# Turned blocks through GpSimd's DMA queue, convolution taps spread over chunks, block-product loads in place: a decoder trunk on one core

## The chip, the cores and the metric

The kernel runs on one core of one Trainium2 chip. The metric is the device time of a whole execution in microseconds. Three executions of the kernel before took 2344.26, 2345.53 and 2347.45 us; their median, 2345.53 us, is the time before. The profile is of one more execution, with its own time, given below.

## The reference, cut to what matters

A decoder trunk of two layers on 256 tokens (BATCH = 1, SEQ = 256, D_MODEL = 2048). Layer 0 mixes tokens by gated linear attention, layer 1 by forgetting attention; both attend to 256 memory tokens besides. After each comes the channel mixer, the part that the change is about: a gated MLP with a hidden width of 5632 and a causal convolution of width 3 over the tokens ahead of the gate.

```python
def causal_dwconv(u, w, b):
    s_ = u.shape[1]
    up = jnp.pad(u, ((0, 0), (CONV_WIDTH - 1, 0), (0, 0)))
    return w[0] * up[:, 0:s_] + w[1] * up[:, 1:s_ + 1] + w[2] * up[:, 2:s_ + 2] + b

def conv_ffn(h, w_up, conv_w, conv_b, w_down):
    u = causal_dwconv(h @ w_up, conv_w, conv_b)
    a, val = split_cols(u, [FFN_HIDDEN, FFN_HIDDEN])
    return (jax.nn.silu(a) * val) @ w_down

def reference(x, mem, norm_mix, norm_ffn, ...):
    mem_n = rmsnorm(mem, norm_mem)
    for i in range(DEPTH):
        ...
        h = rmsnorm(x, norm_ffn[i])
        x = x + conv_ffn(h, ffn_w_up[i], ffn_conv_w[i], ffn_conv_b[i], ffn_w_down[i])
    return rmsnorm(x, norm_final)
```

All inputs are float32.

## The kernel before, in words

**Products.** Every float32 factor is split in two halves, hi (rounded) and lo (the rest), and a product is made of three matmuls: hi by hi, lo by hi, hi by lo. Weights come from memory in units of 128 x 1024 (512 KB): SyncE (SP) issues the load into `raw` (L225), ScalarE (ACT) casts it to `whi` (L230), VectorE (DVE) subtracts to get `wlo` (L231). There are four buffers of each. These steps are issued with high priority, so they run ahead of the rest by as much as the buffers allow.

**The channel mixer.** `ffn` works through the hidden width in three parts (`PARTS`) of 16, 16 and 12 chunks of 128. In each part up panels come first, then down panels over the part's chunks. A panel made by `pair_tm` (L373) has 16 units k = 0 to 15 of weights (12 in the last part's down panel). An up panel (`up_pair`) makes four hidden chunks, as two "turned blocks" of two chunks each; the last four chunks of the third part are made by two single panels (`up`, by way of `panel_tm`, 8 units), one turned block each. A down panel (`down_pair`) takes the part's chunks as input and makes two of the four column blocks of the output, f = 0 or 2; so each of the first two parts ends with panels f=0 and f=2, the last with f=0 and the products of `add_out`.

**Block products.** Two units k and k+1 for which `sums` has an entry are multiplied as a 2 x 2 product of blocks with seven products in place of eight. In up panels this is k = 4 (`SEVEN_UP`), in the down panels of the first two parts it is given by `SEVEN_DOWN`. It needs both units at once in `raw2` (two buffers, loads at L391), differences of the weight blocks on DVE (L397 to L400), and its own casts and low halves (L349, L350), and sums of the input blocks (`token_sums`, tiles `usum` and `dsum`). The loads at L391 are issued with high priority and no other tie.

**A turned block.** Up products leave tokens on the partitions; the convolution wants channels there. DVE scales and adds (L1407) and transposes 32 x 32 blocks (L1382). Then `far_away` (L601) writes the tile of 512 KB to DRAM (L603, the profile's `far<-yu` or `far<-yzu`), and `back` reads it in four DMAs of 128 KB (L608, `fvt<-far` or `yzu<-far`), which put the 32 x 32 blocks in place. All are issued by SP. Two buffers are there for each side (`ys`, `zs`).

**The convolution.** `convolve` reads a turned block z: twelve ACT instructions of 128 x 256 (L1347, L1348, L1349, one of each for each of four quarters), two adds on DVE (L1352), SiLU on ACT (L1353), the product with the gate's other half on DVE (L1355, tile `cv`), and the split of the result into the hi and lo halves of `m` (ACT L484, DVE L485), from which the down panels multiply (tiles `mix`, `A`, `B` in the profile). For a chunk in `SEVEN_DOWN`, `token_sums` follows.

**What sets the order.** Each engine runs its instructions in one fixed order, which a scheduler makes from priorities: work written later comes later, unless it stands under `high_priority`; `issue_after(x)` keeps an instruction behind x. Up panels write their turned blocks to DRAM when they end. `close(left)` does the rest, and is called from hooks at given units: it issues the four reads behind the last load so far, then the whole `convolve`, with DVE's part behind the last `wlo` so far. An up panel closes the two blocks of the panel before it after units 7 and 11; a down panel f=0 those of the last up panel after units 7 and 9; the last part's down panel closes what is open after unit 4; the single panels close one at a time.

## Time and profile before

| | |
|---|---|
| median of three executions | 2345.53 us |
| profiled execution, its own time | 2346.2 us |
| its span | 2344.3 us |
| mean granted clock of TensorE | 0.981 |
| TensorE busy | 2247.9 us (96%) |
| VectorE busy | 1790.5 us (76%) |
| ScalarE busy | 1425.3 us (61%) |
| GpSimd busy | 3.3 us, 15 instructions |

A line of the profile names an engine, the line of the kernel, and what it writes and reads (out<-in). Engines are PE (TensorE, matmuls), PEld (its loads of weights, which overlap), DVE (VectorE), ACT (ScalarE), POOL (GpSimd) and SP (SyncE, whose DMA queue is written SPq). Buffer names are shared by several uses: a turned block that has come back is `fvt` in layer 0 and `yzu` in layer 1. TensorE is busy nearly all the time, so a stretch is judged by how far it is longer than its matmuls need, and by the clock that the throttle granted there (1.00 is full speed). A panel of 16 units can be cut out of the span by the start of its first matmul and that of the next panel's first.

### The profile page before, as it was taken

The page shows a single profiled execution, that of the slowest core. Times are in us where ns is not written, and L with a number is a line of the kernel's source. Part 1 is how long each engine was busy: PE and PEld are TensorE (multiplying, and loading weights), DVE is VectorE, ACT ScalarE, POOL GpSimd, SP SyncE. Part 2 cuts the span into 40 slices and gives each one's busy share as a digit, 9 for nine tenths or more (in the row PEclk, how much of TensorE's full clock was granted, in tenths as well). Part 3 has the DMA queues.
Part 4 walks back from the last instruction along what each step waited for, and adds up shares of the span by engine and source line. Part 5 has one row for each costly group of instructions (what it writes and reads, how often), then busy time and mean ns, then how long its engine had stood idle before and what let it go on. Part 6 is the DMA issues. An engine that isn't in the chain of part 4 may idle for free. (4 is left out here: it accounts for less than half of the span.)

```text
span 2344.3 us, 29896 instructions
## 1 busy us (share of the span) xinstructions
PE 2247.9 (96%) x10317; PEld 1869.6 (80%) x10317; DVE 1790.5 (76%) x2639; ACT 1425.3 (61%) x2258; POOL 3.3 (0%) x15
## 2 busy tenths in 40 slices
PE   9999999999979999799999999999997999899997
PEld 7889888878768777687788998877786878778776
DVE  7668887678878689777687579677897868887856
ACT  6655665557755576656674555556765566754674
POOL 0000000000000000000000000000000000000000
PEclk9999999999989999899999999999998999999998
DMA  9777657867755667566788667677675666756683
GB/s 343 230 219 219 197 190 253 255 203 242 226 183 189 219 216 242 162 216 196 242 255 241 207 208 249 199 242 236 208 247 157 219 203 228 225 179 219 203 256 135
DMA packets 183488, 513.37 MB, mean 219 GB/s; under 512 B 20636, under 2 KB 66344, under 8 KB 183336
## 3 DMA queue, kind: packets, MB, share of 16 engines
q1 hardware_dynamic: 182760, 510.66, 68.8%
q8 instruction: 81, 1.33, 0.2%
q10 hardware_dynamic: 576, 0.79, 0.1%
q14 instruction: 71, 0.58, 0.1%
HBM read 468.63 MB, written 42.74 MB: 218 GB/s over the span
## 5 line engine op out<-in xcount | busy, mean ns | idle before, releaser
L231 DVE TENSOR_TENSOR wlo<-raw,whi 128x1024 fp32r<-128x1024 f32 (+4 forms) x734 | 868.5, 1197 | 343.6 <-ACT whi L230 326.2
L230 ACT ACTIVATE whi<-raw 128x1024 fp32r<-128x1024 f32 (+4 forms) x734 | 751.5, 1039 | 491.2 <-PE acc L334 184.8
L334 PE MATMUL acc<-whi,B 128*128 128x512 f32 (+3 forms) x1376 | 323.9, 371 | 0.0
L334 PEld LDWEIGHTS acc<-whi,B 128*128 128x128 f32 x1376 | 251.1, 188 | 33.1
L349 ACT ACTIVATE whi<-raw 128x1024 fp32r<-128x1024 f32 (+1 forms) x144 | 137.2, 953 | 198.4 <-DVE raw L398 62.4
L373 PE MATMUL acc<-whi,mix 128*128 128x512 f32 x850 | 232.0, 409 | 9.6 <-ACT whi L230 8.3
L350 DVE TENSOR_TENSOR wlo<-raw,whi 128x1024 fp32r<-128x1024 f32 (+1 forms) x144 | 155.7, 1082 | 77.1 <-ACT whi L349 73.7
L373 PEld LDWEIGHTS acc<-whi,mix 128*128 128x128 f32 x850 | 168.9, 200 | 49.3 <-ACT whi L230 10.2
L373 PE MATMUL acc<-whi,B 128*128 128x512 f32 x730 | 191.1, 394 | 8.6 <-ACT whi L230 3.7
L334 PE MATMUL acc<-wlo,B 128*128 128x512 f32 (+3 forms) x688 | 176.0, 371 | 0.0
L373 PEld LDWEIGHTS acc<-whi,B 128*128 128x128 f32 x730 | 138.5, 190 | 39.7 <-ACT whi L230 4.8
L334 PEld LDWEIGHTS acc<-wlo,B 128*128 128x128 f32 x688 | 126.6, 188 | 16.9
L1352 DVE TENSOR_TENSOR tap<-tap,tap 128x1024 f32<-128x1024 f32 x88 | 107.4, 1221 | 18.7 <-ACT tap L1348 12.8
L373 PE MATMUL acc<-wlo,mix 128*128 128x512 f32 x425 | 121.4, 391 | 0.0
L373 PE MATMUL acc<-wlo,B 128*128 128x512 f32 x365 | 105.1, 393 | 0.1
L373 PEld LDWEIGHTS acc<-wlo,mix 128*128 128x128 f32 x425 | 80.7, 190 | 17.3
L373 PE MATMUL ps_s<-whi,mix 128*128 128x512 f32 x334 | 94.2, 394 | 0.0
L373 PE MATMUL ps_s<-whi,B 128*128 128x512 f32 x342 | 94.0, 390 | 0.0
L334 PE MATMUL acc<-whi,mix 128*128 128x512 f32 x336 | 84.2, 390 | 0.0
L373 PEld LDWEIGHTS acc<-wlo,B 128*128 128x128 f32 x365 | 69.0, 189 | 15.4 <-DVE wlo L350 0.5
L373 PEld LDWEIGHTS ps_s<-whi,B 128*128 128x128 f32 x342 | 64.2, 188 | 13.7
L373 PEld LDWEIGHTS ps_s<-whi,mix 128*128 128x128 f32 x334 | 63.3, 190 | 13.7
(417 smaller groups left out, 3670.7 us busy)
## 6 DMA issues: line engine op xcount, KB each, us to landing
raw<-wp SPq DMA_DIRECT2D x743, 512.0 KB, 4.4
fvt<-far SPq DMA_DIRECT2D x100, 128.0 KB, 4.6
raw<-wp SPq DMA_DIRECT2D x32, 384.0 KB, 3.5
yzu<-far SPq DMA_DIRECT2D x96, 128.0 KB, 4.4
far<-yu SPq DMA_DIRECT2D x22, 512.0 KB, 3.4
far<-yzu SPq DMA_DIRECT2D x22, 512.0 KB, 3.4
raw<-wp SPq DMA_DIRECT2D x24, 388.0 KB, 3.7
far<-blk SPq DMA_DIRECT2D x12, 512.0 KB, 4.7
```

Source lines behind the costliest of these rows:

```text
L230: casts.append(S.activation(hi[:, s], raw[:, s], AF.Copy))
L231: lows.append(V.tensor_tensor(lo[:, s], raw[:, s], hi[:, s].bitcast(F32), ALU.subtract))
L334: mm = TE.matmul(acc[b][:, :n], src[kc - base][:, part, b * P : (b + 1) * P], ready[low][:, j * n : (j + 1) * n], start=i == low == part = ...
L349: casts.append(S.activation(hi[:, :n], src, AF.Copy))
L350: lows.append(V.tensor_tensor(lo[:, :n], src, hi[:, :n].bitcast(F32), ALU.subtract))
L373: r = TE.matmul(bank[name], x, w, start=name not in begun, stop=last)
L1352: V.tensor_tensor(t, t, taps[i_][:, :, :, :T], ALU.add)
```

## The change

- `far_away` takes a queue. In the channel mixers the write and the four reads of a turned block are issued on GpSimd's queue, all at once when the block is turned; elsewhere they stay on SP. In all 44 writes and 176 reads move. Blocks of the single panels land in a tile of their own, with the buffers of `raw2`.
- `convolve` is cut into six steps: `taps_of` for each quarter (three ACT instructions, kept behind the last cast so far), `add_taps`, `gated` (their DVE instructions kept behind the last `wlo` so far). A turned block puts its steps in a list `waiting` with the unit from which each may run, 8 units after the block was turned (7 for single panels). `tick(most)` counts units and runs up to `most` steps that are due; up panels run one and two in turn, the others two a unit. A down panel runs down what is left: at most six steps are open after unit 11 of 16, none after unit 13 (7 and 9 of 12 in the last part).
- The loads of a block product stay behind the last load so far.
- The down panels' second block product is that of units 10 and 11, where it was 8 and 9.
- Hooks become one function that is called at every unit; after a block product it is called for both of its units. A closure that nothing called goes away.

The matmuls and the arithmetic of every engine are the same, but for which pair of units is the second block product.

```diff
--- before.py
+++ after.py
@@ -33,7 +33,7 @@
 PARTS = ((0, 16), (16, 32), (32, 44))
 WIDE = ((0, 4, 8, 12), (16, 20, 24, 28), (32, 36))
 SEVEN_UP = (4,)
-SEVEN_DOWN = (4, 8)
+SEVEN_DOWN = (4, 10)
 
 
 LEVELS = (64, 16, 4)
@@ -350,7 +350,7 @@
             lows.append(V.tensor_tensor(lo[:, :n], src, hi[:, :n].bitcast(F32), ALU.subtract))
         return hi, lo
 
-    def pair_tm(units, src, sums, flip, pool, early, late, hooks={}):
+    def pair_tm(units, src, sums, flip, pool, early, late, hook):
 
         bank = {}
         fast, slow = ("p1", "p5", "p7", "p6"), ("p2", "p3", "p4", "x")
@@ -358,6 +358,7 @@
         tags = {n: ("acc", 4) for n in accs}
         tags.update(zip(works, (("o", 1), ("s", 2), ("s", 2), ("t", 1))))
         begun = set()
+        sums = dict(sums)
         n = len(units)
         plan = []
         k = 0
@@ -387,8 +388,9 @@
             if k in sums:
                 with tc.high_priority(offset=AHEAD):
                     ra, rb = [pool.tile([P, NUNIT], F32, name="raw2", tag="raw2", bufs=2) for _ in range(2)]
-                    for t, (off, _, w) in ((ra, units[k]), (rb, units[k + 1])):
-                        loads.append(nc.sync.dma_start(t, wp[off : off + P * w].rearrange("(p n) -> p n", p=P)))
+                    with tc.issue_after(loads[-1].ins):
+                        for t, (off, _, w) in ((ra, units[k]), (rb, units[k + 1])):
+                            loads.append(nc.sync.dma_start(t, wp[off : off + P * w].rearrange("(p n) -> p n", p=P)))
                 st = [[sums[k][:, part, j, :] for part in range(2)] for j in (3, 0, 1, 2)]
                 done = k == end[-1]
                 w1 = split_more(ra[:, :512], 512)
@@ -409,7 +411,8 @@
                 last_mm.append(three("p4", tok(k + 1, 1), [t[:, :512] for t in w4]))
                 if done:
                     early(bank)
-                hooks.get(k + 1, int)()
+                hook(k)
+                k += 1
             else:
                 w = split_unit(units[k])
                 last = k == n - 1
@@ -423,7 +426,7 @@
                         ends.append(r)
                         late(b, h, bank[name])
                 last_mm.append(r)
-            hooks.get(k, int)()
+            hook(k)
 
     def token_sums(r, dst):
 
@@ -597,15 +600,15 @@
                 (nc.scalar if on_act(q, c) else nc.sync).dma_start(
                     dst[32 * c : 32 * (c + 1), q], src[32 * q : 32 * (q + 1), c])
 
-    def far_away(pool, src, n):
+    def far_away(pool, src, n, queue=nc.sync):
 
         far = pool.tile([P, 4 * T], F32, name="far", tag="far", bufs=3)
-        nc.sync.dma_start(far[:, : 4 * n], src[:, : 4 * n])
+        queue.dma_start(far[:, : 4 * n], src[:, : 4 * n])
         blocks = far[:, : 4 * n].rearrange("(q i) (c n) -> c i q n", q=4, c=4)
 
         def back(dst):
             for c in range(4):
-                nc.sync.dma_start(dst[32 * c : 32 * (c + 1), : 4 * n].rearrange("i (q n) -> i q n", q=4), blocks[c])
+                queue.dma_start(dst[32 * c : 32 * (c + 1), : 4 * n].rearrange("i (q n) -> i q n", q=4), blocks[c])
 
         return back
 
@@ -1277,7 +1280,7 @@
                     steps[f](u)
 
 
-    def down_pair(l, p, f, src, sums, flip, pool, temps, then=None, hooks={}):
+    def down_pair(l, p, f, src, sums, flip, pool, temps, hook, then=None):
 
         def early(bank):
             t0, t1 = temps()
@@ -1296,7 +1299,7 @@
             if then is not None:
                 then(f + h, b)
 
-        pair_tm(where["down", l, p, f], src, sums, flip, pool, early, late, hooks)
+        pair_tm(where["down", l, p, f], src, sums, flip, pool, early, late, hook)
 
     def add_out(key, src, then=None, spare=None, last=None, first=0, hooks=None, late=1):
 
@@ -1331,33 +1334,40 @@
             for i in (1, 2):
                 nc.gpsimd.memset(taps[i][:, :, :, :i], 0.0)
             count = [0, 0, 0]
-            open_ = []
             sums = {}
 
             def held(name, i):
                 return fp.tile([P, 2, 4, P], F32R, name=name, tag=f"{name}{i}")
 
-            def convolve(j, i, z, seven):
-
-                for s in range(2):
-                    for c in range(2):
-                        col = (c * 44 + j + s) * 4
-                        w = [cw[:, col + n : col + n + 1] for n in range(4)]
-                        src = z[:, :, 2 * c + s]
-                        S.activation(by_run(taps[0][:, s, c, :]), src, AF.Identity, bias=w[3], scale=w[2])
-                        S.activation(by_run(taps[1][:, s, c, 1:]), src, AF.Copy, scale=w[1])
-                        S.activation(by_run(taps[2][:, s, c, 2:]), src, AF.Copy, scale=w[0])
+            def taps_of(j, s, c, z):
+
+                col = (c * 44 + j + s) * 4
+                w = [cw[:, col + n : col + n + 1] for n in range(4)]
+                src = z[:, :, 2 * c + s]
+                with tc.issue_after(casts[-1].ins):
+                    S.activation(by_run(taps[0][:, s, c, :]), src, AF.Identity, bias=w[3], scale=w[2])
+                    S.activation(by_run(taps[1][:, s, c, 1:]), src, AF.Copy, scale=w[1])
+                    S.activation(by_run(taps[2][:, s, c, 2:]), src, AF.Copy, scale=w[0])
+
+            def add_taps():
+
                 t = taps[0]
-                for i_ in (1, 2):
-                    V.tensor_tensor(t, t, taps[i_][:, :, :, :T], ALU.add)
+                with tc.issue_after(lows[-1].ins):
+                    for n in (1, 2):
+                        V.tensor_tensor(t, t, taps[n][:, :, :, :T], ALU.add)
                 S.activation(t[:, :, 0, :], t[:, :, 0, :], AF.Silu)
+
+            def gated(i, seven):
+
+                t = taps[0]
                 r = fp.tile([P, 2, T], F32, name="cv", tag="cv")
-                V.tensor_tensor(r, t[:, :, 0, :], t[:, :, 1, :], ALU.mult)
-                for s in range(2):
-                    split(m, i + s, r[:, s, :])
-                if seven:
-                    sums[i] = held("dsum", i)
-                    token_sums(r, sums[i])
+                with tc.issue_after(lows[-1].ins):
+                    V.tensor_tensor(r, t[:, :, 0, :], t[:, :, 1, :], ALU.mult)
+                    for s in range(2):
+                        split(m, i + s, r[:, s, :])
+                    if seven:
+                        sums[i] = held("dsum", i)
+                        token_sums(r, sums[i])
 
             def input_sums(k):
 
@@ -1372,24 +1382,36 @@
             def scale(b):
                 return nx.col()[:, b : b + 1]
 
-            def turn(j, i):
+            def turn(j, i, wait, z=None):
 
                 count[0] += 1
                 y = ys[count[0] % 2]
+                z = zs[count[0] % 2] if z is None else z
 
                 def evac(b, a):
                     with tc.high_priority(offset=AHEAD):
                         V.transpose(y[:, :, :, b, :], a.rearrange("p (k c i) -> p c k i", c=4, i=32))
                     if b:
-                        back = far_away(dram, flat(y), T)
-                        open_.append((j, i, back))
+                        far_away(dram, flat(y), T, nc.gpsimd)(flat(z))
+                        steps = [lambda s=s, c=c: taps_of(j, s, c, z) for s in range(2) for c in range(2)]
+                        steps += [add_taps, lambda: gated(i, j < PARTS[-1][0] and i in SEVEN_DOWN)]
+                        waiting.extend((clock[0] + wait, step) for step in steps)
 
                 return evac
 
-            def up_pair(j, i, hooks):
+            waiting, clock = [], [0]
+
+            def tick(most):
+
+                clock[0] += 1
+                for _ in range(most):
+                    if waiting and waiting[0][0] <= clock[0]:
+                        waiting.pop(0)[1]()
+
+            def up_pair(j, i, hook):
 
                 count[2] += 1
-                turns = [turn(j + 2 * h_, i + 2 * h_) for h_ in range(2)]
+                turns = [turn(j + 2 * h_, i + 2 * h_, 8) for h_ in range(2)]
                 u = {}
 
                 def early(bank):
@@ -1407,11 +1429,11 @@
                     V.scalar_tensor_tensor(u[b, h_], a, scale(b), u[b, h_], ALU.mult, ALU.add)
                     turns[h_](b, u[b, h_])
 
-                pair_tm(where["up", l, j], h, up_sums, count[2] % 2, pool, early, late, hooks)
+                pair_tm(where["up", l, j], h, up_sums, count[2] % 2, pool, early, late, hook)
 
             def up(j, i):
 
-                done = turn(j, i)
+                done = turn(j, i, 7, pool.tile([P, 4, 4, 2, 32], F32, name="turn2", tag="raw2", bufs=2))
 
                 def evac(b, a):
                     t = temps(b)
@@ -1420,50 +1442,39 @@
 
                 return panel_tm(("up", l, j), h, evac)
 
-            def close(left):
-
-                while len(open_) > left:
-                    j, i, back = open_.pop(0)
-                    z = zs[count[1] % 2]
-                    count[1] += 1
-                    with tc.issue_after(loads[-1].ins):
-                        back(flat(z))
-                    with tc.issue_after(lows[-1].ins):
-                        convolve(j, i, z, j < PARTS[-1][0] and i in SEVEN_DOWN)
-
-            def closing(*at):
-                return {k: lambda left=len(at) - 1 - i: close(left) for i, k in enumerate(at)}
-
-            def take_first():
-                nx.take()
-                for k in SEVEN_UP:
-                    input_sums(k)
+            def first(k):
+                {2: lambda: nx.land(landing[0]), 3: nx.take, 8: nx.col,
+                 9: lambda: nx.land(landing[1]), 11: nx.take}.get(k, int)()
+                tick(0)
 
             for p, (lo, hi) in enumerate(PARTS):
+                end = p == len(PARTS) - 1
                 for j in WIDE[p]:
-                    hooks = closing(7, 11)
                     if p == 0 and j == lo:
                         for k in SEVEN_UP:
                             input_sums(k)
-                        hooks = {2: lambda: nx.land(landing[0]), 3: nx.take, 8: nx.col,
-                                 9: lambda: nx.land(landing[1]), 11: nx.take}
-                    up_pair(j, j - lo, hooks)
+                    up_pair(j, j - lo, first if p == 0 and j == lo else lambda k: tick(1 + clock[0] % 2))
                 for j in range(lo, hi, 2):
                     if j in WIDE[p] or j - 2 in WIDE[p]:
                         continue
                     step = up(j, j - lo)
                     for u in range(8):
                         step(u)
-                        if u in (2, 5):
-                            close(max(1, len(open_) - 1))
-                end = p == len(PARTS) - 1
+                        tick(2)
                 for f in (0,) if end else (0, 2):
-                    hooks = {4: lambda: close(0)} if end else closing(7, 9) if f == 0 else {}
-                    if end:
-                        hooks[6] = getattr(then, "begin", int)
                     count[2] += 1
+
+                    def hook(k):
+                        tick(2)
+                        if k in (hi - lo - 5, hi - lo - 3):
+                            left = 6 if k == hi - lo - 5 else 0
+                            while len(waiting) > left:
+                                waiting.pop(0)[1]()
+                        if end and k == 6:
+                            getattr(then, "begin", int)()
+
                     down_pair(l, p, f, m, {} if end else sums, count[2] % 2, pool, lambda: (temps(0), temps(1)),
-                              then if end else None, hooks)
+                              hook, then if end else None)
                 sums.clear()
             add_out(("down", l, len(PARTS) - 1), m, then=then, first=2, spare=spare, last=last)
 
```

## The prediction

> **What bounds the kernel now.** First the page's head and first part, then the windows cut at the panel borders, then the waits of TensorE (columns of the waits: total us, times, longest us).
>
> ```profile
> span 2344.3 us, 29896 instructions
> PE 2247.9 (96%) x10317; PEld 1869.6 (80%) x10317; DVE 1790.5 (76%) x2639; ACT 1425.3 (61%) x2258; POOL 3.3 (0%) x15
> ```
>
> TensorE is the bound, so only its idle time and its slow clock can be won: the change removes no matmul. Two panels without a convolution run free of stalls and give the floor of a panel.
>
> ```profile
> 701.10:743.70 42.60, 42.60 (x188) 35.09 (x187) 37.06 (x45) 20.55 (x22) 0.00 (x0) 1.00 0.62 200
> 743.50:786.60 43.10, 43.10 (x191) 35.60 (x190) 28.80 (x31) 21.29 (x24) 0.00 (x0) 1.00 0.62 197
> ```
>
> The first is a down panel (f=2), the second an up panel: length, busy time of PE, PEld, DVE, ACT, POOL, then granted clock, 1.00 in both. Against them stand the panels in which a convolution runs: the four down panels f=0 of the first two parts (first row below, sum of the four), the fourteen up panels after the first of each part's start (first, last, sum), and the two down panels of the last parts.
>
> ```profile
> 640.00:701.20 61.20, 49.05 (x188) 38.38 (x187) 47.77 (x60) 34.39 (x55) 0.00 (x0) 0.86 0.60 187
> ...
> sum 239.40, PE 192.37 PEld 151.90 DVE 186.49 ACT 136.32 POOL 0.00; mean PE 48.09 PEld 37.98 DVE 46.62 ACT 34.08 POOL 0.00
> ```
>
> ```profile
> 505.80:551.20 45.40, 43.52 (x191) 35.58 (x190) 36.27 (x42) 33.89 (x54) 0.00 (x0) 1.00 0.67 213
> ...
> 2169.20:2216.90 47.70, 45.58 (x193) 37.10 (x192) 37.66 (x45) 34.62 (x54) 0.00 (x0) 0.96 0.62 199
> sum 638.80, PE 615.30 PEld 500.23 DVE 525.75 ACT 469.69 POOL 0.00; mean PE 43.95 PEld 35.73 DVE 37.55 ACT 33.55 POOL 0.00
> ```
>
> ```profile
> 1156.80:1195.70 38.90, 35.11 (x146) 27.99 (x145) 25.84 (x31) 27.24 (x49) 0.00 (x0) 0.96 0.74 230
> 2259.80:2302.80 43.00, 37.83 (x146) 30.17 (x145) 24.08 (x29) 25.79 (x46) 0.00 (x0) 0.88 0.68 221
> ```
>
> Excess over the floor: f=0, 239.4 − 4×42.6 = 69.0; up, 638.8 − 14×43.1 = 35.4; last parts, 81.9 − 2×42.6×146/188 = 15.7 (scaled by the matmul records). Together 120 us, the most that this change can touch. The waits name what ends the stalls: casts of the weights on ACT, above all those of the block products (L349).
>
> ```profile
> PE ps_t L373 <- ACT whi L349: 23.8, 8, 5.8
> PE ps_s L373 <- ACT whi L349: 23.6, 6, 6.4
> PE ps_o L373 <- ACT whi L230: 14.5, 8, 2.5
> PE acc L373 <- ACT whi L230: 12.0, 6, 3.1
> ```
>
> Why the casts are late shows in the timeline of the panel at 640.0, ACT first (start, length, idle before and its releaser), then SP.
>
> ```profile
> 655.93 0.60 ACT L1347 ACTIVATE tap<-fvt,cw 128x256 f32<-128x256 f32 x1 [2.00 <-DMA fvt<-far]
> ...
> 659.81 0.59 ACT L1347 ACTIVATE tap<-fvt,cw 128x256 f32<-128x256 f32 x1
> 660.30 1.04 ACT L349 ACTIVATE whi<-raw 128x1024 fp32r<-128x1024 f32 x1
> ...
> 672.77 0.52 ACT L1348 ACTIVATE tap<-fvt,cw 128x256 f32<-128x256 f32 x1 [3.80 <-DMA fvt<-far]
> ...
> 675.98 1.04 ACT L349 ACTIVATE whi<-raw 128x1024 fp32r<-128x1024 f32 x1
> ```
>
> ```profile
> 648.68 1.52 SPq L603 DMA_DIRECT2D far<-yu  x2
> 651.31 1.77 SPq L608 DMA_DIRECT2D fvt<-far  x4
> 655.79 7.19 SPq L391 DMA_DIRECT2D raw<-wp  x2
> 663.03 1.55 SPq L608 DMA_DIRECT2D fvt<-far  x2
> ```
>
> Ten taps stand before the cast at 660.30, eight before that at 675.98; ACT itself first waited 2.00 and 3.80 us for the turned block, and the second block's reads waited on SP behind two loads for a block product that held the queue 7.19 us. What TensorE lost by it, and what the clock then added:
>
> ```profile
> 661.40 1.22 PE L373 MATMUL ps_t<-whi,dsum 128*128 128x512 f32 x2 [4.85 <-ACT whi L349]
> 677.08 2.08 PE L373 MATMUL ps_s<-whi,dsum 128*128 128x512 f32 x4 [4.66 <-ACT whi L349]
> ```
>
> ```profile
> 675.60:685.80 10.20, 7.64 (x17) 5.57 (x18) 7.32 (x9) 9.22 (x15) 0.00 (x0) 0.50 0.37 108
> ```
>
> After such a stall the granted clock is 0.50 for some us. In the last part's panel the taps themselves come late and TensorE waits behind them:
>
> ```profile
> 1164.72 0.60 ACT L1347 ACTIVATE tap<-fvt,cw 128x256 f32<-128x256 f32 x1 [4.70 <-DMA fvt<-far]
> ...
> 1171.00 3.43 PE L373 MATMUL acc<-whi,mix 128*128 128x512 f32 x8 [3.15 <-ACT whi L230]
> ```
>
> **The change, part by part.** The order of the changed program has the same matmuls, casts, taps and DVE instructions, in the same forms; only order and queues differ. The sum is made against the profiled run's own time, 2346.2 us (span 2344.3, so 1.9 around it); the median of the runs shown is 2345.53.
>
> *Turned blocks on POOL's queue.* The 44 far writes and 176 reads leave SP and are issued by POOL as soon as a block is turned. On SP that frees 220 issues; SP is no bound, and gains only in that weight loads never stand behind a waiting read. What an issue on POOL takes, no row shows: POOL has 15 instructions and no DMA. The nearest rows are SP's own issues and the DVE instruction for which POOL might have to wait:
>
> ```profile
> L608 SPq DMA_DIRECT2D fvt<-far x100: 302/430/1367, 514.9 to 1222.0; - x100
> L231 DVE TENSOR_TENSOR wlo<-raw,whi 128x1024 fp32r<-128x1024 f32 (+4 forms) x734 | 868.5, 1197 | 343.6 <-ACT whi L230 326.2 <-PE acc L334 5.6 <-PE acc L259 2.7
> ```
>
> Lower bound 0.43 us (the median), then 0.43 + 1.2 = 1.6, and 0.43 + 2×1.2 = 2.8 if two DVE instructions hold each issue. I take about 1 us, between the first two, with no row nearer. What it may cost: from the first write's issue (648.68, panel start + 8.7) to the first tap (655.93) a block took 7.25 us on SP, so it is in place at + 16. Six more issues are in its way now (two writes, four reads of the block before), each g − 0.43 longer. In the new order ACT casts units 6 to 9 first and comes to the taps near + 19 (seven units of 43.1/16 = 2.7 each). Twelve taps take 5.2 us: from 655.93 to 659.81 nine of them start, one every 0.43. The cast behind them is that of unit 10, which TensorE reaches at 10×2.7 = 27, near + 28 with the stall of unit 4 before it. So a landing up to 28 − 5.2 = + 22.8 costs nothing: (22.8 − 16)/6 + 0.43 = 1.56 us an issue. Above that each microsecond more costs six per panel.
>
> The wait for the write now stands on POOL, behind which only other blocks queue. On the Trainium skill's page "SBUF — State Buffer", section "Who interferes with whom", DVE in a two-port mode locks GpSimd out of SBUF, and its note on the "DVE blocks DMA" trap says that descriptors for a GpSimd DMA then can't be written; tensor_tensor is said to have no such mode. No run here shows POOL's DMA beside DVE yet. By that page these panels, whose DVE rows are tensor_tensor, scalar_tensor_tensor and transposes, would be free of the lock, and the sum stays as it is.
>
> *Convolution spread, block product (4,8) to (4,10), in the f=0 panels.* The first two long stalls (4.85, 4.66) go: taps stand behind casts of coming units. What is late next is DVE and the splits of the last chunks: chunks 12 to 15 of this panel are still made in it, and their splits stand later than before, since their convolution starts 8 ticks after the turn. DVE's work bounds the panel from below: 46.62 us mean, 4 over the floor; from above the old 59.85 (239.4/4). Following the new order with these durations I find about 1 us at unit 4, 1 at unit 10, 4 at unit 12 and 2 to 4 at unit 14, and one slow-clock stretch of 1.5 (3.4 us at half): 53 us, midway between the bounds. Gain 4 × (59.85 − 53) = 27.4; bounds 0 and 53.
>
> *The same in up panels.* The mean excess is 35.4/14 = 2.5 us. The burst of taps no longer precedes a due cast, but DVE's subtractions for the block product at unit 4 follow older convolution work on DVE (37.55 of 45.6 us busy): 1.5 us stays. Gain 14 × 1.0 = 14; bounds 0 and 35.4.
>
> *Last parts.* The reads no longer wait for the hook after unit 4, so the taps come before the cast that waited 3.15 us; a stall of 1.8 stays where chunk 10's split stands behind the next cast, and part of the slow clock. Gain 15.7 − 2×3 = 9.7; bounds 0 and 15.7.
>
> *The single panels' block tile.* It takes a buffer of the block products' loads; after the last pair panel of a layer no block product follows in that mixer, so nobody waits for it: 0.
>
> *Loads for block products in order.* They are issued later than now, but still about four units (11 us) before their use, and a load lands 4.4 us after issue: no cost while those 6 us cover it.
>
> ```profile
> raw<-wp SPq DMA_DIRECT2D x743, 512.0 KB, 4.4
> ```
>
> Sum: 2346.2 − 27.4 − 14 − 9.7 = 2295.1 us.
>
> **The rivals.**
> 1. *POOL's issues are slow* (the other side). At 2.4 us an issue a block lands at 16 + 6×1.97 = + 27.8, 5.0 late: 2.5 over the old 2.5 in fourteen up panels is 35, a half-clock stretch of 1.5 in each is 21, the other gains are lost: 2346 + 56 = 2402. It decides from about 2.2 us, where 14 × 6 × (g − 1.56) eats the 51 gained. For it: no POOL DMA in the trace, and DVE is busy 78% of the f=0 panels (46.62 of 59.85), so an issue that needs DVE to pause waits often. Against it: 10 issues in 43 us leave 4 us for each.
> 2. *The stall only moves to DVE.* Casts of a block product follow DVE's subtractions already; if DVE's order sets the f=0 panels, only 2 us each go there and little elsewhere: 2346 − 10 = 2336. For it: 46.62 us of DVE in 42.6 of matmuls. Against it: DVE idles 13 us in these panels today.
> 3. *All the stalls go.* With DVE's 46.62 left in f=0 and the last parts as forecast: 2346 − 53 − 35 − 10 = 2248. For it: every long wait named ends in an ACT cast. Against it: the late splits above.
> 4. *The change doesn't do what it says*: POOL's reads land no earlier than SP's did, since the write's landing is waited for either way. Then only the 7.19 us hold on SP goes, near 2330; it is in rival 2's chance.
>
> **How the numbers follow.** Forecast 2295 (2278 to 2315): 0.42. Rival 3: 0.11. Rivals 2 and 4: 0.22, of which 0.12 is faster, 0.05 within 0.2% (about what a measurement of this kernel can tell from no change), 0.05 slower. Rival 1: 0.25, all slower. So faster 0.65, same 0.05, slower 0.30. The range goes from rival 3 to between no change and rival 1's time, 2248 to 2385; above it lie POOL issues near 2.4 us and more.
>
> **What would show it.** Right: the f=0 panels near 53 us with no wait over 4.9 on L349; up panels near 44.6; the last parts' near 36; issues on POOL of about 1 us; first taps without idle for a block; half-clock stretches fewer. Wrong: taps that idle for their block in up panels (rival 1); f=0 panels of 57 us or more with DVE busy nearly throughout (rival 2); waits on loads for block products.

## The result and the profile after

Four executions of the changed kernel took 2288.9 to 2291.38 us, median 2289.98; the kernel before, beside it, 2345.8. The ratio is 0.976 with a 95% interval of [0.9745, 0.9779]: faster by 56 us, where 2295.1 was forecast. The profiled execution took 2289.51 us. Its head and first part, from the page:

```profile
span 2287.7 us, 30031 instructions
PE 2230.5 (97%) x10317; PEld 1861.7 (81%) x10317; DVE 1790.0 (78%) x2639; ACT 1416.9 (62%) x2258; POOL 124.3 (5%) x235
```

TensorE has the same 10317 matmuls and is busy 17 us less; since the matmuls are the same, that is taken here as less of the half clock (the mean granted clock rose from 0.981 to 0.990). The other 39 us of the 56.6 by which the span is shorter were its idle time. The windows at the panel borders, cut as in the prediction (length, busy time of PE, PEld, DVE, ACT, POOL, granted clock), first for the four f=0 panels:

```profile
636.10:684.70 48.60, 45.33 (x188) 35.71 (x187) 45.77 (x61) 34.37 (x55) 5.50 (x10) 0.96 0.66 225
...
sum 200.80, PE 183.55 PEld 145.42 DVE 182.12 ACT 135.27 POOL 21.99; mean PE 45.89 PEld 36.35 DVE 45.53 ACT 33.82 POOL 5.50
```

for the fourteen up panels (two of them and the sum):

```profile
505.00:548.10 43.10, 43.10 (x191) 35.62 (x190) 37.02 (x43) 32.67 (x52) 5.63 (x10) 1.00 0.72 236
...
591.30:636.30 45.00, 43.48 (x191) 35.53 (x191) 39.49 (x48) 33.05 (x54) 5.49 (x10) 1.00 0.70 237
...
sum 614.40, PE 607.30 PEld 497.93 DVE 530.07 ACT 464.63 POOL 77.06; mean PE 43.38 PEld 35.57 DVE 37.86 ACT 33.19 POOL 5.50
```

and for the down panels of the two last parts:

```profile
1124.80:1169.90 45.10, 37.29 (x146) 29.93 (x146) 26.01 (x31) 27.54 (x50) 2.74 (x5) 0.89 0.59 189
2203.60:2246.10 42.50, 34.99 (x146) 28.21 (x145) 25.41 (x30) 27.68 (x50) 2.74 (x5) 0.92 0.62 211
```

Against the panels of before: f=0 239.4 to 200.8 (-38.6), up 638.8 to 614.4 (-24.4), last parts 81.9 to 87.6 (+5.7). The waits of TensorE (total us, times, longest) say what is left:

```profile
PE acc L374 <- ACT B L487: 9.3, 2, 6.5
PE acc L374 <- ACT whi L349: 8.2, 6, 1.6
PE acc L374 <- ACT A L487: 4.6, 2, 2.8
PE ps_s L374 <- ACT whi L349: 4.2, 3, 2.8
PE acc L374 <- ACT fvt L1440: 3.9, 1, 3.9
PE acc L374 <- ACT mix L487: 3.9, 1, 3.9
PE ps_t L374 <- ACT whi L349: 3.0, 5, 1.6
...
PE ps_o L374 <- ACT whi L349: 2.2, 1, 2.2
```

Two rows of before, beside those that the prediction shows:

```profile
PE acc L373 <- ACT whi L349: 3.9, 4, 1.8
...
PE ps_o L373 <- ACT whi L349: 2.0, 2, 1.5
```

The 47.4 us that ps_t and ps_s waited for casts of block products (L349) have shrunk to 7.2; on acc and ps_o these waits grew from 5.9 to 10.4. Together 53.3 became 17.6. As much again, 17.8 in these rows, are now waits for splits of the convolution's result (L487), and these are the longest that are left (6.5); 3.9 is for an evacuation (L1440). ACT's timeline shows how an f=0 panel runs now (start, length, idle before):

```profile
649.19 3.89 ACT L230 ACTIVATE whi<-raw 128x1024 fp32r<-128x1024 f32 x4
652.98 0.59 ACT L1348 ACTIVATE tap<-fvt,cw 128x256 f32<-128x256 f32 x1
...
666.58 2.94 ACT L230 ACTIVATE whi<-raw 128x1024 fp32r<-128x1024 f32 x3
...
671.01 0.71 ACT L487 ACTIVATE A<-cv 128x256 fp32r<-128x256 f32 x2
```

Four casts go ahead of the first tap, which doesn't wait for its block. TensorE's only long wait in this panel is for the split at 671.01:

```profile
671.47 3.53 PE L374 MATMUL acc<-whi,A 128*128 128x512 f32 x8 [2.76 <-ACT A L487]
```

GpSimd's issues, from the tile's view (duration in ns, min/median/max):

```profile
L611 POOL DMA_DIRECT2D fvt<-far x80: 550/552/574, 514.0 to 1096.3; - x80
```

### The profile page after: what moved, and what is told of

Same layout as the page of the kernel before. It is cut to its first block, busy times and chain, and to the rows that moved or that the text cites. A ratio compares the mean times of both kernels' runs of the same rounds, so it can differ in the third digit from the quotient of the medians.

```text
span 2287.7 us, 30031 instructions
## 1 busy us (share of the span) xinstructions
PE 2230.5 (97%) x10317; PEld 1861.7 (81%) x10317; DVE 1790.0 (78%) x2639; ACT 1416.9 (62%) x2258; POOL 124.3 (5%) x235
## 5 line engine op out<-in xcount | busy, mean ns | idle before, releaser
L231 DVE TENSOR_TENSOR wlo<-raw,whi 128x1024 fp32r<-128x1024 f32 (+4 forms) x734 | 866.9, 1196 | 321.8 <-ACT whi L230 300.4
L349 ACT ACTIVATE whi<-raw 128x1024 fp32r<-128x1024 f32 (+1 forms) x144 | 136.6, 952 | 208.3 <-PE acc L374 73.4
L374 PE MATMUL acc<-whi,mix 128*128 128x512 f32 x850 | 222.9, 396 | 9.4 <-ACT fvt L1440 3.9
L374 PEld LDWEIGHTS acc<-whi,mix 128*128 128x128 f32 x850 | 161.6, 191 | 45.2 <-ACT fvt L1440 4.3
L374 PEld LDWEIGHTS acc<-wlo,mix 128*128 128x128 f32 x425 | 81.0, 191 | 17.8 <-DVE wlo L350 0.7
L374 PE MATMUL ps_s<-whi,mix 128*128 128x512 f32 x334 | 93.1, 391 | 0.0
L334 PE MATMUL acc<-whi,mix 128*128 128x512 f32 x336 | 84.1, 390 | 0.0
L374 PEld LDWEIGHTS ps_s<-whi,B 128*128 128x128 f32 x342 | 64.2, 188 | 13.5
L374 PEld LDWEIGHTS ps_s<-whi,mix 128*128 128x128 f32 x334 | 63.0, 189 | 13.4
```

The source lines that it names most:

```text
L231: lows.append(V.tensor_tensor(lo[:, s], raw[:, s], hi[:, s].bitcast(F32), ALU.subtract))
L334: mm = TE.matmul(acc[b][:, :n], src[kc - base][:, part, b * P : (b + 1) * P], ready[low][:, j * n : (j + 1) * n], start=i == low == part = ...
L349: casts.append(S.activation(hi[:, :n], src, AF.Copy))
L374: r = TE.matmul(bank[name], x, w, start=name not in begun, stop=last)
```

## The experiments

Twelve kernels ran, each beside the kernel before. For each, this table gives the sums of the windows at its own panel borders (us, from its profiled execution), its median, and the ratio to the kernel before, run beside it, with its interval. "At once" means that a block is read back when it is turned; "tied" that the loads of block products keep their place; the product is the second block product of an f=0 panel.

| kernel | queue | at once | tied | product | spread | 14 up | 4 f=0 | 2 last | median us | ratio |
|---|---|---|---|---|---|---|---|---|---|---|
| before | SP | no | no | 8 | no | 639 | 239.4 | 81.9 | 2345.8 | 1 |
| after | POOL | yes | yes | 10 | yes | 614.4 | 200.8 | 87.6 | 2289.98 | 0.976 [0.9745, 0.9779] |
| e1 | SP | yes | yes | 10 | yes | 612.0 | 197.9 | 78.4 | 2273.86 | 0.970 [0.968, 0.972] |
| e2 | POOL | yes | no | 8 | no | 615.7 | 208.1 | 89.6 | 2300.29 | 0.981 [0.979, 0.984] |
| e3 | POOL | yes | no | 10 | yes | 615.7 | 196.9 | 91.5 | 2287.41 | 0.976 [0.973, 0.979] |
| e4 | POOL | yes | yes | 8 | yes | 614.8 | 232.3 | 91.4 | 2317.81 | 0.989 [0.987, 0.992] |
| e5 | SP | yes | no | 8 | no | 641.3 | 211.0 | 96.9 | 2332.05 | 0.994 [0.992, 0.996] |
| e6 | POOL | yes | yes | 10 | no | 614.9 | 195.2 | 90.6 | 2287.15 | 0.974 [0.972, 0.976] |
| e7 | as after, first single block's steps due later | | | | | 614.8 | 194.0 | 74.8 | 2269.05 | 0.967 [0.965, 0.969] |
| e8 | as e1, first single block's steps due later | | | | | 612.5 | 197.1 | 85.8 | 2282.73 | 0.972 [0.970, 0.974] |
| e9 | SP | no | yes | 8 | no | 642.5 | 236.0 | 81.2 | 2345.41 | 1.000 [0.998, 1.001] |
| e10 | SP | yes | yes | 10 | no | 638.1 | 189.0 | 95.3 | 2305.17 | 0.983 [0.981, 0.985] |
| e11 | as e7, pair panels' steps due after 6 | | | | | 614.8 | 197.3 | 83.7 | 2276.67 | 0.970 [0.968, 0.972] |
| e12 | as after, reads issued in four | | | | | 631.1 | 215.9 | 120.4 | 2345.77 | 1.000 [0.999, 1.001] |

### First: one part undone, or done alone

The theory was the prediction's: what pays is the order on ACT, the spread taps, and the queue only has to bring blocks in time. The rival: the queue pays.

e1, the blocks back on SP:

```diff
-                        far_away(dram, flat(y), T, nc.gpsimd)(flat(z))
+                        far_away(dram, flat(y), T)(flat(z))
```

> The changed kernel with one part undone: the turned blocks' writes and reads go back to SP's queue, issued at once when the block is turned; the spread convolution, the ordered loads and (4, 10) stay. Theory (the order on ACT is what pays, the queue only has to bring blocks in time): the f=0 panels stay near 50 us and the up panels near 44; on SP each block holds the weight loads for the write's landing, some 4 to 5 us, against a lead of four units (10.7 us), so 2290 to 2302 us. Rival (the queue is what pays): weight loads late behind waiting reads, at least half of the 56 us lost again, over 2318 us.

It took 2273.86 us, less than either expected: GpSimd's queue, in the kernel with all the rest, costs about 0.6% (the intervals of e1 and after don't meet). The table shows where: 9 of it in the last parts, 3 each in f=0 and in the first up panel of each layer (96.2 to 93.1 for the two), 2 in the other up panels.

e2, only the blocks on GpSimd's queue, in the kernel before (`convolve` in one piece from the old hooks):

```diff
-                        back = far_away(dram, flat(y), T)
-                        open_.append((j, i, back))
+                        z = zs[count[1] % 2]
+                        count[1] += 1
+                        far_away(dram, flat(y), T, nc.gpsimd)(flat(z))
+                        open_.append((j, i, z))
...
```

> The kernel before with one part of the change alone: the turned blocks are written and read on GpSimd's queue as soon as they are turned; the convolution still runs in one piece from the old hooks, the block products are (4, 8), their loads are untied. Theory: the taps still stand before the due cast, so the stall at the first block product of an f=0 panel (4.85 us) and those of the up panels (2.5 us a panel) stay; what goes is the stall whose taps waited for reads held on SP (4.66 us) with part of the slow clock, 4 times some 6 us: 2315 to 2330 us. Rival (the queue is what pays): 2290 to 2305 us.

2300.29 us, the rival's number. So most of the gain comes without any spreading, and yet e1 shows that it doesn't need this queue either. The two parts overlap; e5, e6, e9 and e10 below part them.

e3, the loads of block products untied:

```diff
-                    with tc.issue_after(loads[-1].ins):
-                        for t, (off, _, w) in ((ra, units[k]), (rb, units[k + 1])):
-                            loads.append(nc.sync.dma_start(t, ...))
+                    for t, (off, _, w) in ((ra, units[k]), (rb, units[k + 1])):
+                        loads.append(nc.sync.dma_start(t, ...))
```

> The changed kernel with one part undone: the loads of block products are no longer kept behind the last load. Theory: with no reads of turned blocks on SP, a load that runs ahead there holds up only weight loads that have a lead of four units: 2288 to 2295 us. Rival: the early loads wait on SP for their two buffers and the weight loads wait behind them, a stall of about 3 us in each of the 18 panels with a block product and a convolution: over 2320 us.

2287.41 us, the same as after: with the blocks gone from SP the tie of these loads is worth nothing.

e4, the second block product at units 8 and 9 again:

```diff
-SEVEN_DOWN = (4, 10)
+SEVEN_DOWN = (4, 8)
```

> The changed kernel with the second block product of the down panels at units 8 and 9 again. Theory: it asks for the sums of chunks 8 and 9 and DVE's differences two units earlier, so the f=0 panels lose about 2 us each and the others nothing: 2296 to 2302 us. Rival: DVE's work there is the same whichever units they are, 2288 to 2293 us.

2317.81 us: 28 us lost, against 8 expected and 3 at most by the rival; the f=0 panels lose 31.5 (232.3). ACT's timeline of e4, and then TensorE's, in the panel that starts at 633.8:

```profile
653.71 0.63 ACT L349 ACTIVATE whi<-raw 128x512 fp32r<-128x512 f32 x1 [4.28 <-DMA raw<-wp]
654.25 0.59 ACT L1348 ACTIVATE tap<-fvt,cw 128x256 f32<-128x256 f32 x1
...
659.40 1.99 ACT L349 ACTIVATE whi<-raw 128x1024 fp32r<-128x1024 f32 x2
```

```profile
660.50 0.73 PE L374 MATMUL acc<-whi,mix 128*128 128x512 f32 x2 [4.21 <-ACT whi L349]
```

In this panel all twelve taps fall between the first cast of the second block product and its second: the stall of before, in a new place. The spread taps are tied to follow the last cast, and where that is the product's first cast they sit inside the product. The 4.28 us belong to it as well: that first cast waits for its load, and the taps wait behind it. In e2, which has the product at 8 and no spreading, these loads are issued as early (13.5 us into its first f=0 panel, here 13.4, so the tie of the loads makes no difference), but there ACT runs a block's twelve taps while they are on their way, from 648.51 to 653.67. Not all of the 4.21 us are the taps' doing: DVE waits for the product's second load until 656.82, so they delay its cast, at 659.40, by 2.6 us at most. The panel's other long waits, 3.35 and 1.68 us, are for the two halves of a split, later on. In the changed kernel, two units later, the same two casts start at 656.46 and 658.67 without a wait for a load. So (4, 10) is no small extra: with the spreading it is what keeps the f=0 panels short.

### Second: at once, or another queue, or the spreading

e5, as e2, but on SP:

```diff
-                        back = far_away(dram, flat(y), T)
-                        open_.append((j, i, back))
+                        z = zs[count[1] % 2]
+                        count[1] += 1
+                        far_away(dram, flat(y), T)(flat(z))
+                        open_.append((j, i, z))
...
```

> The kernel before with one thing changed: a turned block is read back as soon as it is turned, still on SP's queue; convolution in one piece from the old hooks, block products (4, 8), loads untied. The run with the blocks alone on GpSimd's queue gained 42 us, that with all but the queue was 14 to 16 us faster than the whole change. Theory (what pays is that blocks come early; GpSimd's queue itself costs): 2284 to 2302 us. Rival (SP must be relieved of the blocks unless the block products' loads keep their place, since these hold it up to 7 us): 2310 us or more, with waits of casts on late weight loads.

2332.05 us, the rival's side. But not as it said: f=0 falls as in e2 (211.0), while the up panels keep all their excess (641.3).

e6, the whole change but the spreading, which is e2 with these two edits:

```diff
-SEVEN_DOWN = (4, 8)
+SEVEN_DOWN = (4, 10)
...
-                    for t, (off, _, w) in ((ra, units[k]), (rb, units[k + 1])):
-                        loads.append(nc.sync.dma_start(t, ...))
+                    with tc.issue_after(loads[-1].ins):
+                        for t, (off, _, w) in ((ra, units[k]), (rb, units[k + 1])):
+                            loads.append(nc.sync.dma_start(t, ...))
```

> The whole change but the spreading: blocks at once on GpSimd's queue, loads of block products in place, block products (4, 10), and the convolution in one piece from the old hooks. Theory (blocks that come early already place the taps well, and the spreading is what made (4, 8) 28 us slower): (4, 10) gives a few us over the run with the blocks alone, 2285 to 2300 us, so the spreading is worth under 10 us. Rival (spreading pays beside it): 2303 to 2325 us, since with taps in one piece the f=0 panels stay near 52 to 58 us.

2287.15 us, its interval overlapping that of after: beside the other parts the spreading is worth nothing. The run also shows what (4, 10) and the tie bring together without the spreading: f=0 208.1 to 195.2.

e9 is the kernel before with the second of these edits alone, the tie; e10 is e5 with both:

> The kernel before with one thing changed: the loads of a block product stay behind the last load. Reads of turned blocks still come from the old hooks, on SP. Theory (in up panels the taps are late because reads wait on SP behind loads for a block product that run ahead): the fourteen up panels fall from 639 to about 620 us, the f=0 panels lose the stall whose reads were held 7 us, 2305 to 2325 us. Rival (the hooks themselves come too late): up panels stay over 630, 2335 us or more.

> The kernel before with blocks read back at once on SP, block-product loads in place and (4, 10); no GpSimd queue, no spreading. With at-once reads on SP alone the up panels stayed at 641 us, on GpSimd's queue they fell to 615. Theory (it was the untied loads on SP that held the reads): up panels at 612 to 618, f=0 panels near 49 each, 2272 to 2290 us. Rival (on SP the spreading is needed): 2300 us or more, up panels over 625.

e9 is at 1.000, e10 at 2305.17 with 638.1 us of up panels: the theory that untied loads on SP hold the reads of the up panels falls twice. e10's f=0 panels are the shortest of all, 47.3 us each, without GpSimd's queue and without the spreading. What e10's up panels lack can be seen beside e2's. ACT and SP of e10, in the up panel that starts at 503.2, and TensorE:

```profile
512.40 3.64 SPq L609 DMA_DIRECT2D fvt<-far  x8
517.14 11.59 SPq L225 DMA_DIRECT2D raw<-wp  x4
```

```profile
516.83 0.60 ACT L1348 ACTIVATE tap<-fvt,cw 128x256 f32<-128x256 f32 x1 [0.97 <-DMA fvt<-far]
...
522.66 1.05 ACT L230 ACTIVATE whi<-raw 128x1024 fp32r<-128x1024 f32 x1
```

```profile
523.76 0.73 PE L373 MATMUL ps_o<-whi,B 128*128 128x512 f32 x2 [1.89 <-ACT whi L230]
```

and POOL, then ACT, of e2 in the same panel:

```profile
510.79 4.38 POOL L608 DMA_DIRECT2D fvt<-far  x8 [2.58 <-DMA far<-yu]
```

```profile
515.78 2.95 ACT L230 ACTIVATE whi<-raw 128x1024 fp32r<-128x1024 f32 x3
518.62 0.59 ACT L1347 ACTIVATE tap<-fvt,cw 128x256 f32<-128x256 f32 x1
```

In neither is the block late: ACT waits 0.97 us for it in e10, not at all in e2. The difference is the order on ACT: in e2 three casts stand ahead of the taps, in e10 the taps ahead of the same casts. Why the scheduler orders them so stays open. The trace gives no reason to hold these casts back. Of the four loads that were then in the buffers of `raw`, e10's ACT casts one ahead of the taps (at 514.79) and three behind them, and all four had been issued by 507.08, ahead of the reads at 512.40. The spreading changes the order by force, since it ties each group of taps behind a cast. In e1, on SP, two casts stand between the twelve taps of that panel:

```profile
518.70 1.05 ACT L230 ACTIVATE whi<-raw 128x1024 fp32r<-128x1024 f32 x1
...
522.23 1.05 ACT L230 ACTIVATE whi<-raw 128x1024 fp32r<-128x1024 f32 x1
```

TensorE does not wait there, and e1's up panels are at 612.0. The up panels need one of the two, and either is enough: 612 to 616 in each kernel that has GpSimd's queue or the spreading (but e12), 638 to 643 in the four that have neither. Each kernel with one of them also reads blocks back at once; without that neither was run.

### Third: the last parts, and a faster version

In the first layer's panel of the last part, TensorE waits in after as follows (ACT's timeline, then TensorE's; the third row of TensorE is from the second layer's panel):

```profile
1128.57 1.71 ACT L1349 ACTIVATE tap<-turn,cw 128x256 f32<-128x256 f32 x4 [5.18 <-DMA turn<-far]
...
1132.30 0.67 ACT L1440 ACTIVATE fvt<-acc,ny 128x512 f32<-128x512 f32 x1
```

```profile
1133.01 1.22 PE L374 MATMUL acc<-whi,mix 128*128 128x512 f32 x2 [3.93 <-ACT fvt L1440]
1161.75 3.78 PE L374 MATMUL acc<-whi,mix 128*128 128x512 f32 x8 [3.88 <-ACT mix L487]
...
2238.78 3.61 PE L374 MATMUL acc<-whi,B 128*128 128x512 f32 x8 [6.52 <-ACT B L487]
```

ACT waits 5.18 us for the first single panel's block, and only then evacuates the second single panel (L1440), whose bank TensorE wants; so that panel's block, too, is late, and its split at the end. The spreading is not what brings this: e2, without it, has the same wait in the same place (4.48 us), and its last parts take 89.6. e7 lets the first block's steps become due after 14 units:

```diff
-                done = turn(j, i, 7, pool.tile(...))
+                done = turn(j, i, 14 if j % 4 == 0 else 7, pool.tile(...))
```

> The changed kernel, but the steps of the first single panel's block become due 14 units after its turn, where it was 7, so that ACT evacuates the second single panel before it comes to those taps. Theory (in the last parts' panels TensorE waits since ACT, in its order, waits some 5 us for a block before it evacuates, and everything after is late): the two last panels go from 45.0 and 42.5 to 36 to 39 us, 2276 to 2284 us in all. Rival (the wait moves to the splits of chunks 8 to 11 in the same panels): within 3 us of 2290.

ACT and the windows of e7:

```profile
1117.77 0.69 ACT L1440 ACTIVATE fvt<-acc,ny 128x512 f32<-128x512 f32 x1 [0.32 <-PE acc L334]
...
1126.26 0.59 ACT L1348 ACTIVATE tap<-turn,cw 128x256 f32<-128x256 f32 x1
```

```profile
1118.90:1156.80 37.90, 35.28 (x146) 27.98 (x145) 25.39 (x31) 26.70 (x48) 2.75 (x5) 0.95 0.64 217
2187.10:2224.00 36.90, 34.80 (x146) 28.10 (x145) 24.98 (x30) 26.80 (x48) 2.76 (x5) 0.95 0.71 249
```

The evacuation now comes first, the taps find their block without idle, and the two panels fall from 87.6 to 74.8. At 2269.05 us e7 is below the range expected and faster than both kernels of the case; it has the lowest median of all, though its interval meets that of e1. Its f=0 panels are 6.8 shorter too, which the edit does not explain; e3, which differs from after only by the tie, is at 196.9, so some of this may come and go with small differences of order.

e8 makes the same edit in e1:

```diff
-                done = turn(j, i, 7, pool.tile(...))
+                done = turn(j, i, 14 if j % 4 == 0 else 7, pool.tile(...))
...
-                        far_away(dram, flat(y), T, nc.gpsimd)(flat(z))
+                        far_away(dram, flat(y), T)(flat(z))
```

> The changed kernel with blocks on SP's queue, as in the run that was fastest so far, and the first single panel's steps due after 14 units. Theory: what is lost in the last parts there (38.7 and 39.8 us against a floor of 33) goes down by 1 to 2 us each: 2269 to 2274 us. Rival: the block's steps come so late that chunk 8 is late in the down panel: 2276 us or more.

2282.73 us, the rival's side: no gain on e1 (0.972 against 0.970, the intervals overlap), and the last parts go from 78.4 to 85.8. ACT now idles for a weight load, which on SP stands behind a block's reads, and TensorE waits above all for the split of the block whose steps were put off, 3.47 us in the first layer and 6.85 in the second:

```profile
1125.57 1.06 ACT L230 ACTIVATE whi<-raw 128x1024 fp32r<-128x1024 f32 x1 [5.20 <-DMA raw<-wp]
```

```profile
1152.02 3.54 PE L374 MATMUL acc<-whi,mix 128*128 128x512 f32 x8 [3.47 <-ACT mix L487]
```

So SP was the faster queue in one pair of kernels only, e1 against after; with e7's order (e8), and without the spreading (e5 against e2, e10 against e6), it was the slower one. What GpSimd's queue costs can't be given as one number.

e11 is e7 with the pair panels' steps due two units earlier:

```diff
-                turns = [turn(j + 2 * h_, i + 2 * h_, 8) for h_ in range(2)]
+                turns = [turn(j + 2 * h_, i + 2 * h_, 6) for h_ in range(2)]
```

> The changed kernel with the first single panel's steps due after 14 units, which ran in 2269 us, and the steps of pair panels due after 6 units in place of 8. Theory (the 2.8 us at unit 12 of each f=0 panel is a split that comes late because its steps start late; blocks land some 3 us before their taps): 1 to 2 us less in each f=0 panel and no new idle taps, 2260 to 2267 us. Rival (DVE sets the time of that split, or taps now wait for their blocks ahead of due casts): 2269 us or more.

2276.67 us, the rival's side: no gain on e7 (0.970 against 0.967, the intervals meet), f=0 3.3 longer, last parts 8.9. The stall at unit 12, which stands in three of e7's four f=0 panels, isn't won by an earlier start. In three of e11's four it is 1.16 us for ACT's half of the split and then 1.84 for DVE's half (L488), with DVE busy without a pause for the 5.7 us before it. So with the earlier start DVE's order sets the end of this stall.

e12 issues each read on GpSimd's queue in four:

```diff
-                queue.dma_start(dst[32 * c : 32 * (c + 1), : 4 * n].rearrange("i (q n) -> i q n", q=4), blocks[c])
+                to = dst[32 * c : 32 * (c + 1), : 4 * n].rearrange("i (q n) -> i q n", q=4)
+                for q in range(4) if queue is nc.gpsimd else (slice(0, 4),):
+                    queue.dma_start(to[:, q], blocks[c][:, q])
```

> The changed kernel with each read of a turned block issued in four of 32 KB: 16 issues a block on GpSimd's queue where there were 4, the same bytes. At 0.55 us each a pair of blocks takes 18 us of issues more than 13 us longer than now, which is as if an issue took some 2.2 us. Theory (the prediction's bound of 1.56 us an issue): the second block of a panel lands some 13 us later, ACT idles before its taps, the up panels get about 2 to 4 us longer: 2315 to 2350 us. Rival (the second block's steps stand four units later, so most of that is covered): under 2305 us.

2345.77 us: the whole gain is gone, inside the range expected, but hardly for the reason given. The up panels lose 1.2 us each (631.1), not 2 to 4, and of all taps one waits for its block, 1.3 us; f=0 loses 15 and the last parts 33, where TensorE waits for two splits in each panel (the first layer's):

```profile
1174.57 3.78 PE L374 MATMUL acc<-whi,mix 128*128 128x512 f32 x8 [10.12 <-ACT mix L487]
1191.74 3.78 PE L374 MATMUL acc<-whi,mix 128*128 128x512 f32 x8 [9.42 <-ACT mix L487]
```

The order of the program differs from that of after (ACT runs 66 to 68 instructions in an f=0 panel, where it ran 51 to 55), presumably because the scheduler reckons with the longer issues; so this run prices slow issues together with the order made for them, not the wait alone.

## Why the prediction was right, and where not

- *The bound and the stalls.* Right. TensorE's idle time behind ACT's casts and the half clock after it were what could be won; of the 120 us of excess 57.3 went (38.6 + 24.4 - 5.7).
- *The sum.* 51.1 forecast, 56.7 by the two profiled executions (2346.2 - 2289.51). It is nearer than its terms: f=0 gave 38.6 for 27.4, the up panels 24.4 for 14, the last parts lost 5.7 where 9.7 was to be gained. Errors of +11.2, +10.4 and -15.4 cancel, so how near the total came is luck.
- *f=0.* The size was off: 50.2 us a panel for 53. Unit 12's late split came in three of the four panels (2.76, 1.82 and 2.75, for 4), the one forecast at unit 14 (2 to 4) in none; the panel at 1715.5 has a wait of 2.76 for a cast of the second block product and one of 2.58 for a low half of weights (DVE, L231) instead. The clock's part differs from panel to panel (granted 0.93 to 0.96). The cause was put in the wrong part: the gain was booked under the spreading with (4, 10). e2 has neither and gains 31.3 in these panels, and e5, the same on SP, 28.4: what both do is read blocks back at once. (4, 10) with the tie brings 12.9 more (e6), the spreading nothing on top, and without (4, 10) it costs 24 (e4 against e2). Rival 2, the stall that only moves to DVE, did not come in the changed kernel: DVE was busy for 45.5 of 50.2 us.
- *Up panels.* The step "the burst of taps no longer precedes a due cast" holds. Some 1.9 us stay in the fourth up panel of a part (45.0 us above, against a floor of 43.1); the forecast let 1.5 stay in all fourteen, where the mean is (614.4 - 14×43.1)/14 = 0.8. And the burst was still there in e2, twelve taps in a row; it only stood behind three casts.
- *The last parts.* The step that failed: "the taps come before the cast that waited 3.15 us". They did come early, so early that ACT stood before them waiting for the block (5.18 us), with an evacuation behind. e7 shows it: 12.8 us by one due time. The prediction asked of the wait on GpSimd's queue what stands behind it, but not of this one on ACT.
- *GpSimd's issues.* 0.55 us, below the 1 us taken, which had no row nearer than SP's issues; rival 1 did not come. Its point of decision was put at 2.2 us an issue. With four issues of 0.50 us for each read (2.0 together) the gain is just gone (e12), but in the panels where rival 1 did not look for it, so the agreement proves little. On the Trainium skill's page "SBUF — State Buffer", section "Who interferes with whom", tensor_tensor has no two-port mode; with both inputs in SBUF it contends with GpSimd's reads, but, as the page infers, not with the writing of descriptors. The trace agrees: the 80 issues took 550 to 574 ns, with DVE busy 45.77 of 48.60 us in the f=0 panel quoted above.
- *Loads in order, cost nothing.* Right for the changed kernel (e3); the tie alone is worth nothing in the kernel before either (e9).

## What to carry to other kernels

A DMA queue can also change what the scheduler does elsewhere: with the same reads on a second queue ACT did casts and taps in another order, and that was worth 23 to 26 us here (up panels of e10 against e6, e5 against e2). When several parts of a change each seem to explain the gain, run each alone and all but each: here two of them were substitutes in the up panels, one (the tie of the loads) was worth nothing where it was tried alone or left out, and one repaired what another broke. An instruction that waits in an in-order engine is priced by what stands behind it: letting one evacuation go ahead of taps that waited 5 us gave 12.8 us in two panels.

## What the runs showed of the hardware

A DMA issue on GpSimd's queue took 0.55 us at 128 KB, against 0.43 on SP, and depends little on the bytes (e12, min/median/max in ns at 32 KB, and at 512 KB for the writes):

```profile
L613 POOL DMA_DIRECT2D fvt<-far x320: 496/498/518, 514.3 to 1127.8; - x160
...
L606 POOL DMA_DIRECT2D far<-yu x22: 542/571/677, 510.4 to 1151.2; - x22
```

The clock fell after a stall of 2.76 us already: the 3.4 us of after that follow the stall at 671.47 run at 0.58.

```profile
668.00:671.40 3.40, 0.71 (x2) 0.28 (x2) 3.40 (x4) 3.40 (x8) 0.00 (x0) 1.00 0.37 118
671.40:674.80 3.40, 3.33 (x9) 2.33 (x10) 3.40 (x7) 3.24 (x7) 0.00 (x0) 0.58 0.90 287
```

The Trainium skill's page "TensorE: Matmul & The Clock Gate", Part 1, gives an idle window of about 3.4 us for this. The trace shows a shorter one here: TensorE was busy for 0.71 of the 3.4 us before. In e10 a stall of 1.89 us (the one before 523.76 above) was enough: the 3.4 us from 523.7 on ran at 0.71.
